# Buffers that wait by tile, combinations in other places and sooner, and a plain block first, in a two-layer decoder kernel

## The chip, the core and the metric

The kernel runs on one core of one Trainium2 chip. The core has a matrix engine (TensorE, in the profile PE, with its weight loads apart as PEld), VectorE (DVE), ScalarE (ACT), GpSimd (POOL) and SyncE (SP), which issues DMAs. DMAs are issued on SP's, ACT's and POOL's queues. The metric is the device time of one execution in microseconds (us), the median of the runs.

## The reference

Two decoder layers on 256 tokens of width 2048, in float32. Layer 0 mixes tokens with gated linear attention (GLA), layer 1 with sliding-window attention over a shared K and V. Each is followed by an MLP with a squared ReLU. Cut to what matters here:

```python
def sqrelu_mlp(h, w1, w2):          # w1: 2048 x 8192, w2: 8192 x 2048
    u = jax.nn.relu(h @ w1)
    return (u * u) @ w2
...
for layer in range(2):
    u = rmsnorm(h, norm_mix[layer])
    h = h + (gla_mixer(u, ...) if layer == 0 else swa_sink_mixer(u, ...))   # both end with  o @ w_o
    h = h + sqrelu_mlp(rmsnorm(h, norm_mlp[layer]), mlp_w1[layer], mlp_w2[layer])
```

## The kernel before

**Products in halves.** Every matrix product is made with both operands split in two: a rounded half (`wh`, `ah`) and the remainder (`wl`, `al`). Three matmuls, `ah*wh`, `ah*wl` and `al*wh`, make up one. A weight block is 512 x 512 (1 MB). It is loaded into a `ws`, `wx` or `wy` buffer; `halve` (L106) casts it on ACT to `wh` (L115) and subtracts on DVE for `wl` (L116), two instructions of each per block. `wp` holds three `ws`, four `wh` and three `wl`. A *plain* block (`Seven.plain`, L238) serves two token tiles with 24 matmuls; a *product* (`Seven.product`, L227) has 12.

**Seven products for eight.** A 2 x 2 arrangement of blocks is multiplied with seven products instead of eight (class `Seven`, L187). For that, sums of activations are formed (`combinations`, L685: four operands, each with its two halves) and sums of weight blocks. The weight sums are made in part by DMA: `load_x` (L211) loads a block in two halves into `wx`, and later adds another onto it with an accumulating DMA on POOL's queue (L216); the first load goes to SP's queue (L218). The order of the products and plain blocks is a string: a single digit is a product, two digits `ij` are a plain block of row `i` and column `j`, `e` and `a` take results out, `x` adds a sum on DVE. Product 1 needs `wx` and the activation's column block 0; plain block 31 needs column block 3.

**The order of the work.** The kernel is written for a tool that places each instruction by its priority in the order of the text, and draws every wait on buffers itself. Loads, casts and remainders of weights are moved up by `high_priority(offset=WPRI)`. Other steps are put off by hand: `later(n, fn)` (L73) runs `fn` at the n-th next `tick()`; a product has one tick, a plain block two.

**From mixer to MLP.** `residual` (L847) multiplies the mixer's output by `w_o`, column blocks 0 and 1 plain and 2 and 3 by seven products in the order `1 21 31 3 7 e 5 20 30 6 2 4`. Its operands are made by `combine_act` (L892) at ticks `COMB`. As a column block is complete, `add_to` (L823) adds it to the residual stream `xs` (L826), and `operands` (L814) turns it with PE transposes (`back`, L810) and scales it into the MLP's activation `act` (ACT L322, DVE L323). Column block 3 is complete after product 6, column block 2 after product 4, the last. `keep_act` (L906) forms the combinations that the MLP needs for every quarter, in two halves `b`, at ticks `KEEP` after the plain columns: sums `xu` (L903), differences `xe` (L688), rounded `xo` (ACT L694) and their remainders (DVE L688). It writes them to DRAM (`kept`, L912, on POOL's queue).

**The MLP.** `mlp` (L932) goes through the hidden width in four quarters `g`. In each, `fetch_sums` (L943) fetches `kept` into `cmb` on POOL's queue, two calls of `two_columns` (L949) make four column blocks of the hidden layer, and `seven` (L1052) multiplies them by `w2`. `two_columns` takes a `wx` from the pool `mp` (two buffers); `wy` is in `mp` too.

**Pools.** Buffers live in pools: `gp` and `g2` in layer 0's mixer, `sp` and `s2` in layer 1's, `mp` in the MLP. A pool opened after another is closed lies on its bytes. In the tool's default (`reuse_waits="pool"`), all tiles of the new pool wait for every user of the pools whose bytes it lands on. A `tag` is a group of buffers of one size within a pool. For a partition, in bytes: in layer 0, `mlev` 189728 to 197920 (two buffers), `z` and two `og` to 202016, four `v` to 210208, four `g` to 218400, two `oh` (with `xu`) to 222496, two `ol` (with `xe`) to 226592; `wx0`, `wgh` and `AT` below. In layer 1, `kh` and `kl` 174208 to 182400, two `qhl` 190720 to 198912, two `qTt` 198976 to 207168, two `sc` to 215360, two `po` (with `xu`) 215616 to 219712. In the MLP, two `wx` 195840 to 212224 and `wy` to 220416.

Of the kernel before, what the change touches and what calls it, by code (L numbers as in the profile page):

```python
# [8 lines left out]
F32 = mybir.dt.float32  # L9
F32R = mybir.dt.float32r  # L10
# [6 lines left out]
P = 128  # L17
# [4 lines left out]
C = 512  # L22
# [18 lines left out]
MX = 2  # L41
COMB = (1, 3)
ORDERS = "1 21 3 7 31 e 5 20 30 6 2 4", "21 1 31 3 7 e 5 20 30 6 2 4"
KEEP = 7, 10
OPS = 7, 9
SQ = (3, 2)
ATT = (5, 3), (9, 6), (10, 8), (11, 10)
# [3 lines left out]
def yoco_kernel(ctx: ExitStack, tc: tile.TileContext, x, norms, mlp_w1, mlp_w2, a_w_in, w_glr, w_gate, a_g_o, a_w_o,  # L51
                kv_w_k, kv_w_v, kv_g_k, b_w_q, b_g_q, b_sinks, b_w_o, out):
    nc = tc.nc
# [19 lines left out]
    def later(n, fn):  # L73
        due.setdefault(now[0] + n, []).append(fn)
# [112 lines left out]
    class Seven:  # L187

        def __init__(self, block, act, es, wx, wy=None):
            self.at, self.act, self.wx, self.banks = block, act, wx, {}
            self.es, self.wy = es, wy

        def block(self, i, j):
            return self.at(i, j).rearrange("(k p) n -> p k n", p=P)
# [14 lines left out]
        def load_x(self, i, j, more=True):  # L211
            with tc.high_priority(offset=WPRI):
                for n in range(2):
                    o, a = self.wx[n], self.block(i, j)[:, 2 * n:2 * n + 2]
                    if more:
                        nc.gpsimd.dma_start(out=o, in_=a, accum_op=ALU.add)  # L216
                    else:
                        nc.sync.dma_start(out=o, in_=a.bitcast(F32))  # L218

        def op(self, i):  # L220

# [195 lines left out]
    wx0 = gp.tile([P, 2, C], F32, name="wx0")  # L417
# [35 lines left out]
    g2 = ga.enter_context(tc.tile_pool(name="g2", bufs=2))  # L453
# [66 lines left out]
    AT = gp.tile([P, 3, H, P], F32, name="AT")  # L520
# [164 lines left out]
    def combinations(os, bs, us, es, sf):  # L685

        ua, ub = us
        sub = lambda o, i, j: nc.vector.tensor_sub(out=o, in0=i, in1=j)  # L688
        sub(es[:, 0], ua[:, :, P:], ub[:, :, P:])
        sub(es[:, 1], ua[:, :, :P], es[:, 0])  # L690
        sub(sf[:, 0], ub[:, :, :P], es[:, 1])
        sub(sf[:, 1], ua[:, :, :P], ua[:, :, P:])
        for o, e in zip(os, (es[:, 0], es[:, 1], sf[:, 0], sf[:, 1])):
            nc.scalar.copy(out=o[:, 0, bs], in_=e)  # L694
            sub(o[:, 1, bs], e, o.bitcast(F32)[:, 0, bs])
# [151 lines left out]
    def residual(w, act, gains, first, room, kept):  # L847
# [20 lines left out]
        for b in range(2):  # L868
            later(KEEP[b], lambda b=b: keep_act(acts[0], b, room, kept))
        v, wx = room["v"](), room["wx"]()  # L870
# [29 lines left out]
    def sums(act, bs, room):  # L900
        us = [room["u"]() for _ in range(2)]
        for c, u in enumerate(us):
            nc.vector.tensor_add(out=u, in0=act[c][0].bitcast(F32)[:, bs], in1=act[c][1].bitcast(F32)[:, bs])  # L903
        return us

    def keep_act(act, b, room, kept):  # L906

        bs = slice(2 * b, 2 * b + 2)
        os = room["o"](b)
        combinations(os, slice(0, 2), sums(act, bs, room), *(room["e"]() for _ in range(2)))  # L910
        for i, o in enumerate(os):
            nc.gpsimd.dma_start(out=kept[i // 2][:, i % 2, :, bs], in_=o.bitcast(F32))  # L912
# [3 lines left out]
    def new_kept(n):  # L916
        return [dp.tile([P, 2, 2, 4, P], F32, name=f"kept{n}{i}") for i in range(2)]

    kept = new_kept(0)

    (actm,), rm = residual(a_w_o[0], acto, (G_MLP0,), True, {
        "v": lambda: g2.tile([P, C], F32, name="vp", tag="vp", bufs=1),
        "wx": lambda: [wx0, g2.tile([P, 2, C], F32, name="wx1", tag="mlev")],
        "es": lambda: [g2.tile([P, 2, 4, P], F32R, name="cmb1", tag="mlev"),
                       wgh.rearrange("p (a k n) -> p a k n", a=2, k=4)],
        "u": lambda: g2.tile([P, 2, T], F32, name="xu", tag="oh"),
        "e": lambda: g2.tile([P, 2, 2, P], F32, name="xe", tag="ol"),
        "o": lambda b: [g2.tile([P, 2, 2, P], F32R, name="xo", tag="vg"[b], bufs=4) for _ in range(4)]}, kept)
    ga.close()


    def mlp(w1, w2, act, r, gains, kept):  # L932
        mx = ExitStack()
        mp = mx.enter_context(tc.tile_pool(name="mp", bufs=2))
        sq, nr = new_norm() if gains else (None, None)
        acts = [{} for _ in gains]
        vs = [mp.tile([P, C], F32, name=f"v{n}", bufs=1) for n in range(2)]
# [8 lines left out]
                with tc.high_priority(offset=WPRI):  # L946
                    nc.gpsimd.dma_start(out=a.bitcast(F32), in_=o)

        def two_columns(col, es, hs, put, order):  # L949


            x = mp.tile([P, 4, C], F32, name="wx", tag="wx")
            add = lambda o, i, j: nc.vector.tensor_add(out=o, in0=i, in1=j)
            sub = lambda o, i, j: nc.vector.tensor_sub(out=o, in0=i, in1=j)
            h, ef = {}, []

            def relu(o, i, t):
                nc.scalar.activation(out=o, in_=i, func=AF.Relu, scale=r[:, t:t + 1])

            def turn(j, t, h):  # L960
                tp = bank([P, 4, P], "tp")
                for k in range(4):
                    nc.tensor.transpose(out=tp[:, k, :], in_=h[:, k * P:(k + 1) * P], identity=ident)  # L963
                put(j, slice(t * P, (t + 1) * P), tp)

            def p1(p):
                h["v"] = hs("v")
                nc.scalar.mul(out=h["v"], in_=p, mul=-1.0)

            def p7(p):  # L970
                h["22"] = hs("22")
                nc.scalar.copy(out=h["22"], in_=p)

            def p5(p):
                h["21"] = hs("p5")
                nc.scalar.copy(out=h["21"], in_=p)

            def p56(p):
                x12, x21 = hs("12"), hs("21")
                v, x22, x5, h["21"] = h["v"], h["22"], h["21"], x21  # L980
                add(v, p, v)
                add(x12, ef[0], v)
                relu(x12, x12, 0)
                later(3, lambda: turn(1, 0, x12))
                sub(x22, v, x22)
                add(x22, ef[1], x22)
                relu(x22, x22, 1)
                later(3, lambda: turn(1, 1, x22))
                sub(x21, x5, v)

            def p2(p):
                relu(h["v"], p, 0)
                later(1, lambda: turn(0, 0, h["v"]))

            def p4(p):
                add(h["21"], p, h["21"])
                relu(h["21"], h["21"], 1)
                later(1, lambda: turn(0, 1, h["21"]))

            z = Seven(lambda i, j: w1[i * C:(i + 1) * C, col[j]:col[j] + C], act, es,  # L1000
                      [x[:, 2 * i:2 * i + 2] for i in range(2)],
                      lambda: mp.tile([P, 4, C], F32, name="wy", tag="wy", bufs=1))
            z.run({"p1": p1, "p7": p7, "ef": lambda e, f: ef.extend((e, f)), "p5": p5, "p56": p56, "a": p2, "c": p4},
                  order)

# [188 lines left out]
        for g in range(4):  # L1194
            w = w2[g * D:(g + 1) * D]
            us, uf = {}, {}
            if g:
                op = new_ops()
            sums, es = new_sums()
            fetch_sums(sums)  # L1200
            if g == 0:
                op = new_ops()
            for c in range(2):
                uf[c] = mp.tile([P, 4, T], F32, name="u", tag="u")

            def put_uf(c, tt, tp, uf=uf):
                nc.scalar.activation(out=uf[c][:, :, tt], in_=tp, func=AF.Square)

            two_columns([g * D + c * C for c in range(2)], es, h_ops(), put_uf,
                        "1 21 3 7 5 31 x 20 e 6 2 30 a 4" if g else "1 31 21 3 7 5 x 20 e 6 2 30 a 4")  # L1210
            for odd in range(2):
                later(OPS[odd], lambda odd=odd, op=op, uf=uf: combine(op, odd, uf))

            def put_us(j, tt, tp, us=us):
                c = 3 - j
                if c not in us:
                    us[c] = new_act()
                ah, al, _ = us[c]
                nc.scalar.activation(out=ah[:, :, tt], in_=tp, func=AF.Square)
                nc.scalar.activation(out=tp, in_=tp, func=AF.Square)  # L1220
                nc.vector.tensor_sub(out=al[:, :, tt], in0=tp, in1=ah.bitcast(F32)[:, :, tt])

            two_columns([g * D + c * C for c in (3, 2)], es, h_rest(), put_us, "1 21 3 7 5 31 x 20 e 6 2 30 a 4")
            for n in range(2):
                seven(w, n, op, us, g, acts, gains, sq, nr)
# [4 lines left out]


    sa = ExitStack()
    sp = sa.enter_context(tc.tile_pool(name="sp", bufs=1))
    s2 = sa.enter_context(tc.tile_pool(name="s2", bufs=2))

    own = sp.tile([P, P], F32, name="own")
    nc.gpsimd.memset(own, 1.0)
# [26 lines left out]
    kh = sp.tile([P, 4, NT, P], F32R, name="kh")  # L1264
    kl = sp.tile([P, 4, NT, P], F32R, name="kl")
# [146 lines left out]
    for g in range(4):  # L1412
# [3 lines left out]
    kept = new_kept(1)  # L1416
# [3 lines left out]
        "es": lambda: [s2.tile([P, 2, 4, P], F32R, name="cmb1", tag="qTt") for _ in range(2)],  # L1420
        "u": lambda: s2.tile([P, 2, T], F32, name="xu", tag="po"),
        "e": lambda: s2.tile([P, 2, 2, P], F32, name="xe", tag="pv"),
        "o": lambda b: [a[:, i] for a in [s2.tile([P, 2, 2, 2, P], F32R, name="xo", tag="qhl") for _ in range(2)]
                        for i in range(2)]}, kept)
    sa.close()
    mlp(mlp_w1[1], mlp_w2[1], actm, rm, (), kept)


# [41 lines left out]
```

## Time and profile before

| what | value |
|---|---|
| time, median of 3 runs | 2047.86 us (2046.93 to 2048.99) |
| the profiled execution | 2049.62 us |
| its span, first to last instruction | 2047.9 us |
| mean granted PE clock | 0.993 |
| busy: PE, DVE, ACT, POOL | 2007.1, 1774.1, 1320.7, 203.6 us |
| moved by DMA | 444.02 MB, mean 217 GB/s |

A row of the order in time has the start in us from the span's start, the time taken, engine, line, operation, written tile `<-` read tile, and shape; `x2` counts merged instructions; the bracket is the engine's idle time before it and what ended that. `SPq` is the queue on which SyncE issues DMAs. In a list of waits the columns are: us in total, number, longest. In a table of stretches each engine has busy us and a count, followed by the granted PE clock, the busy share of the DMA engines and GB/s. Matmul ends are modelled, and a wait for several things is put down to the one that came last.

### The profile page before, as it was taken

The page shows a single profiled execution, that of the slowest core. Times are in us where ns is not written, and L with a number is a line of the kernel's source. Part 1 is how long each engine was busy: PE and PEld are TensorE (multiplying, and loading weights), DVE is VectorE, ACT ScalarE, POOL GpSimd, SP SyncE. Part 2 cuts the span into 40 slices and gives each one's busy share as a digit, 9 for nine tenths or more (in the row PEclk, how much of TensorE's full clock was granted, in tenths as well). Part 3 has the DMA queues.
Part 4 walks back from the last instruction along what each step waited for, and adds up shares of the span by engine and source line. Part 5 has one row for each costly group of instructions (what it writes and reads, how often), then busy time and mean ns, then how long its engine had stood idle before and what let it go on. Part 6 is the DMA issues. An engine that isn't in the chain of part 4 may idle for free.

```text
span 2047.9 us, 25613 instructions
## 1 busy us (share of the span) xinstructions
PE 2007.1 (98%) x9578; PEld 1656.0 (81%) x9578; DVE 1774.1 (87%) x1928; ACT 1320.7 (64%) x1732; POOL 203.6 (10%) x223
## 2 busy tenths in 40 slices
PE   9999999989999999999999999979999999999999
PEld 9988888768878888888887878758888888888887
DVE  6688787879889998989999677979898988998998
ACT  6746666557656657656766677647666656755765
POOL 1251110100000000000001121110000000000000
PEclk9999999989999999999999999989999999999999
DMA  8445776787787687778765543787678678778764
GB/s 284 144 155 179 222 206 206 212 268 218 227 248 244 207 270 226 231 254 253 205 206 166 165 144 125 198 273 225 227 250 241 207 255 255 212 227 256 233 220 129
DMA packets 223372, 444.02 MB, mean 217 GB/s; under 512 B 8352, under 2 KB 18864, under 8 KB 221200
## 3 DMA queue, kind: packets, MB, share of 16 engines
q1 hardware_dynamic: 194752, 376.73, 53.9%
q0 software_dynamic: 25408, 63.79, 15.4%
q10 hardware_dynamic: 3088, 1.88, 0.3%
q8 instruction: 75, 1.23, 0.2%
q14 instruction: 49, 0.40, 0.1%
HBM read 436.07 MB, written 6.29 MB: 216 GB/s over the span
## 4 chain that ended last, share of the span: by engine, by line
PE 66%; issue 16%; DVE 8%; DMA 7%; ACT 3%; POOL 1%; ACTq 0%; SPq 0%; POOLq 0%; DVEq 0%
PE acc L82 49%; PE ms L82 11%; DMA wx<-in_mlp_w_dram 4%; PE tp L82 4%; DVE wl L116 3%; DMA wx<-in_b_w_o_dram 1%; PE tp L963 1%; ACT wh L115 1%; ACT sc L1350 1%; DMA wx<-in_a_w_o_dram 1%; POOL wx L216 0%; DMA ws<-in_a_w_in_dram 0%; PE tp L1282 0%; DVE xs L1107 0%; DVE st L1344 0%
## 5 line engine op out<-in xcount | busy, mean ns | idle before, releaser
L82 PE MATMUL acc<-wh,act 128*128 128x512 f32 x3104 | 1000.3, 395 | 13.1 <-ACT wh L115 12.5
L115 ACT CAST wh<-ws 128x1024 fp32r<-128x1024 f32 x568 | 594.3, 1052 | 335.3 <-PE acc L82 213.7
L116 DVE TENSOR_TENSOR wl<-ws,wh 128x1024 fp32r<-128x1024 f32 x568 | 697.0, 1240 | 91.5 <-ACT wh L115 87.6
L82 PEld LDWEIGHTS acc<-wh,act 128*128 128x128 f32 x3104 | 583.7, 189 | 138.7 <-ACT wh L115 13.6
L82 PE MATMUL acc<-wl,act 128*128 128x512 f32 x1552 | 607.9, 392 | 8.0 <-DVE wl L116 8.0
L115 ACT CAST wh<-wx 128x1024 fp32r<-128x1024 f32 x288 | 302.6, 1052 | 214.8 <-PE acc L82 139.6
L116 DVE TENSOR_TENSOR wl<-wx,wh 128x1024 fp32r<-128x1024 f32 x288 | 347.0, 1220 | 87.5 <-ACT wh L115 84.1
L82 PEld LDWEIGHTS acc<-wl,act 128*128 128x128 f32 x1552 | 292.8, 189 | 70.7 <-DVE wl L116 11.8
L82 PE MATMUL ms<-wh,act 128*128 128x512 f32 x512 | 166.4, 393 | 0.0
L82 PE MATMUL acc<-wh,ops 128*128 128x512 f32 (+1 forms) x392 | 123.3, 386 | 0.1
L82 PE MATMUL acc<-wh,op 128*128 128x512 f32 x384 | 123.4, 389 | 0.0
L82 PEld LDWEIGHTS ms<-wh,act 128*128 128x128 f32 x512 | 96.2, 188 | 19.5
L82 PE MATMUL tp<-wh,cmb 128*128 128x512 f32 x320 | 105.1, 389 | 0.0
L82 PE MATMUL ms<-wl,act 128*128 128x512 f32 x256 | 99.7, 389 | 0.0
L82 PE MATMUL acc<-wh,cmb 128*128 128x512 f32 x296 | 96.1, 391 | 0.0
L82 PE MATMUL acc<-act,wh 128*128 128x256 f32 x512 | 95.5, 285 | 0.5 <-ACT wh L380 0.5
L1070 POOL DMA_DIRECT2D wx<-in_mlp_w_dram x16 | 20.6, 1290 | 652.9 <-DVE wl L116 652.9
L82 PEld LDWEIGHTS acc<-wh,ops 128*128 128x128 f32 x392 | 73.2, 188 | 15.0 <-ACT wh L115 0.6
L82 PEld LDWEIGHTS acc<-wh,op 128*128 128x128 f32 x384 | 72.1, 188 | 14.9
L82 PEld LDWEIGHTS acc<-act,wh 128*128 128x128 f32 x512 | 80.6, 191 | 1.0 <-ACT wh L380 0.8
L82 PE MATMUL acc<-wl,ops 128*128 128x512 f32 (+1 forms) x196 | 76.3, 389 | 3.1 <-DVE wl L116 3.1
L116 DVE TENSOR_TENSOR wl<-wy,wh 128x1024 fp32r<-128x1024 f32 x64 | 76.0, 1219 | 1.3 <-ACT wh L115 1.3
(284 smaller groups left out, 2494.0 us busy)
## 6 DMA issues: line engine op xcount, KB each, us to landing
ws<-in_mlp_w_dram SPq DMA_DIRECT2D x192, 1024.0 KB, 5.6
ws<-in_a_w_in_dram SPq DMA_DIRECT2D x42, 1024.0 KB, 5.1
wy<-in_mlp_w_dram SPq DMA_DIRECT2D x32, 1024.0 KB, 6.2
cmb<-kept POOLq DMA_DIRECT2D x16, 1024.0 KB, 5.4
wx<-in_mlp_w_dram SPq DMA_DIRECT2D x32, 512.0 KB, 6.0
wx<-in_mlp_w_dram POOLq DMA_DIRECT2D x32, 512.0 KB, 6.8
wx<-in_mlp_w_dram SPq DMA_DIRECT2D x16, 1024.0 KB, 5.3
wx<-in_mlp_w_dram POOLq DMA_DIRECT2D x16, 1024.0 KB, 9.5
```

The lines of the kernel that those rows point to most:

```text
L82: nc.tensor.matmul(o, lhsT=l, rhs=r, start=start, stop=stop, **kw)
L115: nc.scalar.copy(out=wh[:, js, :o], in_=w)
L116: nc.vector.tensor_sub(out=wl[:, ks, :o], in0=w, in1=wh.bitcast(F32)[:, js, :o])
L963: nc.tensor.transpose(out=tp[:, k, :], in_=h[:, k * P:(k + 1) * P], identity=ident)
L1070: nc.gpsimd.dma_start(out=ws, in_=block(i, j).rearrange("(k p) n -> p k n", p=P), accum_op=ALU.add)
L1350: nc.scalar.activation(out=sc[:, h], in_=sc[:, h], func=AF.Exp, bias=nmx[:, h:h + 1], scale=f[:, h:h + 1], accum_out=su[:, h:h + 1])
```

## The change

- The pools `mp`, `sp` and `s2` are opened with `reuse_waits="tile"`: each of their tiles waits only for the users of earlier tiles on its own bytes.
- In layer 0, `keep_act`'s `xo` are taken from tag `g` for both halves (before: `v` for the first, `g` for the second), and the second half of residual's `wx` is a part of `AT` (before: an `mlev` buffer).
- In layer 1, `keep_act`'s `xo` are parts of `kh` and `kl` (before: `qhl` buffers).
- `keep_act` runs at ticks 5 and 8 (before: 7 and 10).
- In the first quarter of each MLP, the first `two_columns` starts with plain block 31 and then product 1 (before: product 1, then 31). There the first load of `wx` is issued on POOL's queue (before: SP's).

```diff
-KEEP = 7, 10
+KEEP = 5, 8
...
-        def __init__(self, block, act, es, wx, wy=None):
+        def __init__(self, block, act, es, wx, wy=None, queue=nc.sync):
             self.at, self.act, self.wx, self.banks = block, act, wx, {}
-            self.es, self.wy = es, wy
+            self.es, self.wy, self.queue = es, wy, queue
...
                     if more:
                         nc.gpsimd.dma_start(out=o, in_=a, accum_op=ALU.add)
                     else:
-                        nc.sync.dma_start(out=o, in_=a.bitcast(F32))
+                        self.queue.dma_start(out=o, in_=a.bitcast(F32))
...
-        os = room["o"](b)
+        os = room["o"]()
...
-        "wx": lambda: [wx0, g2.tile([P, 2, C], F32, name="wx1", tag="mlev")],
+        "wx": lambda: [wx0, AT.rearrange("p a h n -> p (a h n)")[:, :2 * C].rearrange("p (a n) -> p a n", a=2)],
...
-        "o": lambda b: [g2.tile([P, 2, 2, P], F32R, name="xo", tag="vg"[b], bufs=4) for _ in range(4)]}, kept)
+        "o": lambda: [g2.tile([P, 2, 2, P], F32R, name="xo", tag="g", bufs=4) for _ in range(4)]}, kept)
...
-        mp = mx.enter_context(tc.tile_pool(name="mp", bufs=2))
+        mp = mx.enter_context(tc.tile_pool(name="mp", bufs=2, reuse_waits="tile"))
...
-        def two_columns(col, es, hs, put, order):
+        def two_columns(col, es, hs, put, order, queue=nc.sync):
...
-                      lambda: mp.tile([P, 4, C], F32, name="wy", tag="wy", bufs=1))
+                      lambda: mp.tile([P, 4, C], F32, name="wy", tag="wy", bufs=1), queue)
...
-                        "1 21 3 7 5 31 x 20 e 6 2 30 a 4" if g else "1 31 21 3 7 5 x 20 e 6 2 30 a 4")
+                        "1 21 3 7 5 31 x 20 e 6 2 30 a 4" if g else "31 1 21 3 7 5 x 20 e 6 2 30 a 4",
+                        nc.sync if g else nc.gpsimd)
...
-    sp = sa.enter_context(tc.tile_pool(name="sp", bufs=1))
-    s2 = sa.enter_context(tc.tile_pool(name="s2", bufs=2))
+    sp = sa.enter_context(tc.tile_pool(name="sp", bufs=1, reuse_waits="tile"))
+    s2 = sa.enter_context(tc.tile_pool(name="s2", bufs=2, reuse_waits="tile"))
...
-        "o": lambda b: [a[:, i] for a in [s2.tile([P, 2, 2, 2, P], F32R, name="xo", tag="qhl") for _ in range(2)]
-                        for i in range(2)]}, kept)
+        "o": lambda: [a[:, 2 * i:2 * i + 2] for a in (kh, kl) for i in range(2)]}, kept)
```

## The prediction

> **What bounds the kernel now.** I read the page first, then what TensorE (PE) waits for, then the engines' order in time at the places where it waits.
>
> ```profile
> PE 2007.1 (98%) x9578; PEld 1656.0 (81%) x9578; DVE 1774.1 (87%) x1928; ACT 1320.7 (64%) x1732; POOL 203.6 (10%) x223
> ```
>
> PE is busy for 98% of the span, so an edit that leaves its work alone can only win what PE waits and what it loses to a lower clock. The list of PE's waits shows nearly all of it at two places of one kind: where residual() hands over to mlp(), once per layer. I call them T1 (around 410 us) and T2 (around 1352 us). Columns: us in total, times, longest. First 400 to 424, then 1340 to 1366:
>
> ```profile
> PE acc L82 <- ACT wh L115: 5.7, 1, 5.7
> PE acc L82 <- DVE wl L116: 3.4, 4, 1.6
> PE tp L810 <- DVE act L323: 2.1, 1, 2.1
> PE tp L810 <- DVE xs L826: 1.1, 1, 1.1
> ```
>
> ```profile
> PE acc L82 <- ACT wh L115: 6.8, 1, 6.8
> PE acc L82 <- DVE wl L116: 3.5, 3, 1.9
> PE tp L810 <- DVE act L323: 2.1, 1, 2.1
> ```
>
> That is 12.3 us at T1 and 12.4 us at T2, 24.7 in all. A second loss is the clock after a wait. In the table of stretches PEclk is the granted clock:
>
> ```profile
> 424.00:436.00 12.00, 12.00 (x49) 9.75 (x48) 10.61 (x10) 7.12 (x10) 3.24 (x3) 0.89 1.08 318
> 1340.00:1352.00 12.00, 8.98 (x31) 6.64 (x30) 12.00 (x20) 4.75 (x10) 2.89 (x4) 0.86 0.61 213
> ...
> 1364.00:1376.00 12.00, 11.48 (x42) 9.05 (x42) 10.40 (x11) 8.46 (x11) 3.76 (x3) 0.80 1.07 296
> ```
>
> The missing clock times 12 us gives 1.3, 1.7 and 2.4 us, 5.4 together. What can be won at most is therefore 24.7 + 5.4 = 30.1 us.
>
> The longest wait is named as ACT, but ACT waits too. PE and ACT at T1, in order of time (start, us, engine, line; in brackets the idle time before):
>
> ```profile
> 411.07 1.06 PE L810 MATMUL tp<-ident,xs 128*128 128x128 f32 x8 [1.07 <-DVE xs L826]
> 414.29 1.94 PE L810 MATMUL tp<-ident,xs 128*128 128x128 f32 x8 [2.15 <-DVE act L323]
> 421.97 0.80 PE L82 MATMUL acc<-wh,act 128*128 128x512 f32 x1 [5.74 <-ACT wh L115]
> ```
>
> ```profile
> 420.87 1.04 ACT L115 CAST wh<-wx 128x1024 fp32r<-128x1024 f32 x1 [6.28 <-DMA wx<-in_mlp_w_dram]
> 421.82 0.83 ACT L322 ACTIVATE act<-tp,gT 128x256 fp32r<-128x256 f32 x2
> ```
>
> PE has finished residual's products at about 410.0; the MLP's first product starts at 421.97, since its weight block wx has only just landed. SyncE issued that block here, at T1 and T2:
>
> ```profile
> 412.56 0.88 SPq L218 DMA_DIRECT2D wx<-in_mlp_w_dram  x2
> ```
>
> ```profile
> 1353.57 0.88 SPq L218 DMA_DIRECT2D wx<-in_mlp_w_dram  x2
> ```
>
> Both stand right behind residual's last work. The pool mp lies on the bytes of the pools closed before it, and by pool each of its tiles waits for every user of those. At T2 PE does the same:
>
> ```profile
> 1348.30 0.78 PE L82 MATMUL acc<-wl,act 128*128 128x512 f32 x1 [1.90 <-DVE wl L116]
> ...
> 1363.57 0.80 PE L82 MATMUL acc<-wh,act 128*128 128x512 f32 x1 [6.80 <-ACT wh L115]
> ```
>
> The waits for wl come from VectorE (DVE), which is full at the end of residual. DVE at T2:
>
> ```profile
> 1337.46 1.23 DVE L116 TENSOR_TENSOR wl<-wx,wh 128x1024 fp32r<-128x1024 f32 x1 [1.46 <-ACT wh L115]
> 1338.60 0.69 DVE L903 TENSOR_TENSOR xu<-act 128x512 f32<-128x512 f32 x1
> ...
> 1345.69 1.43 DVE L688 TENSOR_TENSOR xo<-xe,xo 128x256 fp32r<-128x256 f32 x4
> 1347.03 2.35 DVE L116 TENSOR_TENSOR wl<-wx,wh 128x1024 fp32r<-128x1024 f32 x2
> ...
> 1350.50 1.28 DVE L826 TENSOR_TENSOR xs<-vp,xs 128x512 f32<-128x512 f32 x2
> ```
>
> The second half of keep_act (two xu, four xe, four xo: about 2 x 0.6 + 8 x 0.34 = 3.9 us) runs just ahead of the last product's wl and of the additions that complete column block 3 (L826).
>
> **Waits by tile.** Now a tile of mp waits only for users of its own bytes. By the addresses of the kernel before (the change adds no tag and no size), mp's first wx lies on the second mlev buffer, the og buffers and one v buffer in layer 0. The change takes residual's wx1 out of mlev (to AT) and the xo of keep_act's first half out of v (to g). What is left on those bytes is the xr of turn_x, last read here:
>
> ```profile
> 359.57 0.49 PE L800 MATMUL tp<-ident,xr 128*128 128x128 f32 x3
> ```
>
> In layer 1 the first wx lies on a qhl buffer and the two qTt buffers. The xo leave qhl for kh and kl; the qTt hold operands 2 and 3 of residual's seven products, read for the last time here:
>
> ```profile
> 1325.23 0.39 PE L82 MATMUL acc<-wh,cmb 128*128 128x512 f32 x1
> ```
>
> So the first wx can be issued some 52 us earlier at T1 (412.6 - 360) and 28 us earlier at T2 (1353.6 - 1325.2). A landing takes under 10 us at both places (412.56 to 420.87), so wx is there before residual ends and the waits of 5.7 and 6.8 us for it go. The second wx and wy stay on SyncE and lie on g, oh and sc, po buffers that residual uses to its end; SyncE has by then issued the three ws blocks that fit, so nothing useful stands behind them. For sp and s2 I take zero: what they set free is POOL's masks and constants, which no engine waits for at that place.
>
> **The queue.** The first wx moves from SyncE to POOL, past residual's accumulating loads, the writes of keep_act and the fetch of cmb. At T1 it stands alone, 20 us ahead of the next accumulating loads. At T2 it comes just behind them:
>
> ```profile
> 1324.55 2.43 POOL L216 DMA_DIRECT2D wx<-in_b_w_o_dram  x2 [20.58 <-DVE wl L116]
> ```
>
> They feed the cast ahead of 1337.46, which is on the path. If 1 MB more shares the DMA engines at the 318 GB/s of 424 to 436, they land up to 1.05/0.318 = 3.3 us later; if it queues behind them, 0. A gain I exclude, since nothing is taken off. I take 1 us, nearer to the second, as both stand in one queue.
>
> Does POOL as issuer cost something? Loads of 1 MB from both queues, with the median time to landing last:
>
> ```profile
> wy<-in_mlp_w_dram SPq DMA_DIRECT2D x32, 1024.0 KB, 6.2
> cmb<-kept POOLq DMA_DIRECT2D x16, 1024.0 KB, 5.4
> ```
>
> By these rows nothing. The Trainium skill, page "SBUF — State Buffer", section "SBUF: two separate sides", speaks against the move: it says that descriptors of a load issued from POOL are written through a port that VectorE can lock, so that the load stands still while VectorE works. By that rule wx would come later here, beside a DVE that is full; it is given a chance below.
>
> **Combinations sooner (KEEP 7, 10 to 5, 8).** Two ticks are one plain block or two products. No work goes away. DVE fills idle time with it that it has while it waits for casts: 1.46 us at T2 (row 1337.46), and between 385 and 400:
>
> ```profile
> DVE wl L116 <- ACT wh L115: 3.6, 2, 2.1
> ```
>
> So column block 3 is complete 1.46 us sooner at T2 and 3.6 us sooner at T1, and the last products' wl no longer stand behind xo, so that the 3.4 and 3.5 us of PE's waits for wl mostly go. In the middle of residual the earlier combinations run beside wl that are ahead of PE; wl has priority, and each combination holds DVE for 0.34 to 0.6 us, so I take nothing for it.
>
> **Plain block 31 first.** It needs no wx, only a ws block already loaded, but column block 3's operand act[3], which residual forms at its very end. So what is late next is the way from DVE's additions to act[3]. DVE at T1:
>
> ```profile
> 410.85 0.68 DVE L873 TENSOR_TENSOR xs<-xs,vp 128x512 f32<-128x512 f32 x1
> 411.63 0.69 DVE L826 TENSOR_TENSOR xs<-acc,xs 128x512 f32<-128x512 f32 x1
> 412.25 0.92 DVE L323 SCALAR_TENSOR_TENSOR act<-tp,gT,act 128x256 fp32r<-128x256 f32 x2
> ```
>
> The additions to block 3 end as L873 starts, at 410.9; the first slice of act[3] is ready at 412.25 + 0.46 = 412.7: 1.8 us for transposes, scaling and remainder. The two wl of block 31 (2.35 us, the price of row 1347.03) may stand ahead of the additions or behind them.
>
> **The sum.**
> - T1: 410.9 - 3.6 + (0 to 2.35) + 1.8 = 409.1 to 411.5 for the MLP's first matmul, instead of 421.97: 10.5 to 12.9, middle 11.7.
> - T2: 1350.50 + 1.28 = 1351.8; 1351.8 - 1.46 + (0 to 2.35) + 1.8 = 1352.1 to 1354.5, instead of 1363.57: 9.1 to 11.5, middle 10.3.
> - Clock: a wait of some 3 to 4 us stays at each place, and with it the slow start of the MLP (1.3 and 2.4 us); the 1.7 us before 1352 go with the wait at 1348.30.
> - The accumulating loads at T2: -1.
>
> 11.7 + 10.3 + 1.7 - 1 = 22.7 us. The profiled execution took 2049.62 us with a span of 2047.9; 2049.62 - 22.7 = 2026.9. The median of the runs lies 1.76 below that execution (2047.86), which gives 2025. Nothing should be given back later: the MLP's loads, which now crowd the DMA engines (share 1.08 and 1.07 in the rows above), are spread over a longer time, and DVE, busy for 87% of the span, has room to catch up 2 us.
>
> **Rivals.**
> - *wx is late all the same*, because POOL's queue puts it behind the writes of keep_act, or its bytes hold another late user. Then block 31 alone fills the wait. Twelve matmuls take 2.72 us:
>
> ```profile
> 1385.85 2.72 PE tp L82 x12
> ```
>
>   so its 24 take 5.4, and both places together win 10.9: 2049.62 - 10.9 - 1.76 = 2037. For it: POOL works in order, and keep_act's writes wait for DVE. Against it: the bytes are free so early that the load should be ahead of them. Chance 0.10, and 0.03 more for the page's rule, by which the load would be starved with the same result; the rows of wy and cmb speak against that.
> - *Nothing changes*: the allocator moves other tiles onto those bytes, or waits by tile are not applied, and PE runs the product first as before. Then only the earlier combinations count, 0 to 4 us: about 2046. Chance 0.08.
> - *Slower*: ACT works in order, and at 421.82 the row above shows scaling for act standing behind a cast that waits for wx. If the same happens to act[3], block 31 cannot start before wx either. With wx issued on POOL behind keep_act's writes and the fetch, later than 412.56 and 1353.57 (that is the point from which it decides) by some 2 us, and the scaling and remainder (0.83 + 0.46) behind it, each place loses 3 to 4 us: about 2049.62 + 7 - 1.76 = 2055. Chance 0.07.
> - *All of it goes*, the waits and the slow clock: 2049.62 - 30.1 - 1.76 = 2018. This is the lower end of the forecast's own range.
>
> **How the numbers follow.** The forecast, 2018 to 2033, has a chance of 0.68; wx late 0.13; a smaller gain in between for other reasons 0.04. The range of 2018 to 2038 holds these; above it lie no change and slower with 0.15. About 0.2%, or 4.1 us, is what a measurement of this kernel can tell from no change. Faster by more: 0.85; same: 0.08; slower: 0.07.
>
> **What would show it.** Right: the first wx is issued on POOL's queue near 360 and 1326; the cast of wx no longer waits for a DMA; PE's waits between the last product of residual and the MLP's first matmul shrink to 3 to 4 us at each place, named DVE act or xs; no xo stands ahead of the last wl. Wrong, in the step of the loads: a wait for wx of several us after block 31. Wrong, in the combinations: new waits for wl between 365 and 395 or 1305 and 1340. Wrong as a whole: the MLP's first matmul of layer 0 later than 416 after as much work as before, or the rest of the span longer by what the two places win.

## The result, and the profile after

| | before | after |
|---|---|---|
| median of 20 runs each, same chip | 2047.9 us (2044.42 to 2050.26) | 2043.31 us (2040.71 to 2047.47) |
| the profiled execution | 2049.62 us | 2041.34 us |
| its span | 2047.9 us | 2039.6 us |

The ratio is 0.9979, with an interval of 0.9973 to 0.9986: the change saves 0.14 to 0.27%, about 4.6 us, and not 22.7. The profiled execution of before lies 1.7 us above its median and that of after 2.0 below, so the two traces differ by 8.3 us, more than the medians do.

PE's line on the page of after, and its waits from 400 to 440 and from 1330 to 1380 (us in total, times, longest):

```profile
PE 2007.4 (98%) x9578; PEld 1656.9 (81%) x9578; DVE 1774.5 (87%) x1928; ACT 1321.1 (65%) x1732; POOL 203.4 (10%) x227
```

```profile
PE acc L82 <- ACT wh L115: 3.6, 2, 3.4
PE tp L810 <- DVE xs L826: 2.4, 1, 2.4
PE tp L82 <- DVE xs L872: 1.8, 1, 1.8
...
PE acc L82 <- ACT wh L115: 4.4, 2, 4.0
PE tp L810 <- DVE xs L826: 2.9, 1, 2.9
PE tp L82 <- DVE xs L872: 1.0, 1, 1.0
```

PE's work is the same to 0.3 us. At T1 the waits sum to 7.8 us (12.3 before), at T2 to 8.3 (12.4). The waits for wl at residual's end are gone, and a wait of a new kind has come (L872: DVE's addition that reads product 5 out of its accumulator, bank D, which product 6 needs). A wait for ACT's wh is still the longest, but it has another place. PE in order of time; first the MLP's first matmul of layer 0 and of layer 1, and behind each the place where PE stops next:

```profile
413.36 0.50 PE L82 MATMUL acc<-wh,act 128*128 128x512 f32 x1
...
424.89 0.79 PE L82 MATMUL acc<-wh,act 128*128 128x512 f32 x1 [3.43 <-ACT wh L115]
...
1348.94 0.50 PE L82 MATMUL acc<-wh,act 128*128 128x512 f32 x1
...
1362.56 0.50 PE L82 MATMUL acc<-wh,act 128*128 128x512 f32 x1 [3.97 <-ACT wh L115]
```

The MLP starts at 413.36 instead of 421.97: 8.6 us won. Then PE runs through block 31 and the first six matmuls of product 1, and stops between the halves of product 1. What is left after that is read from one and the same piece of work in both chains, layer 1's attention between T1 and T2 (start, us, what):

```profile
1267.60 8.25 PE acc L82 x36
```

```profile
1262.73 8.25 PE acc L82 x36
```

The first is before, the second after: 4.87 us remain of T1's 8.6. T2's start is 1363.57 - 1348.94 = 14.63 us earlier, of which 4.87 come from T1, so T2 wins 9.8; the two spans differ by 8.3, so 3.4 of T2's 9.8 remain at the end. In these two traces 18.4 us are won at the two starts and about 10 given back.

**What stands in front of the second half of product 1.** ACT and DVE of after at T1:

```profile
415.58 1.05 ACT L115 CAST wh<-wx 128x1024 fp32r<-128x1024 f32 x1
...
423.43 0.47 ACT L322 ACTIVATE act<-tp,gT 128x256 fp32r<-128x256 f32 x1 [2.85 <-DVE act L323]
423.80 1.03 ACT L115 CAST wh<-wx 128x1024 fp32r<-128x1024 f32 x1
```

```profile
417.80 0.48 DVE L323 SCALAR_TENSOR_TENSOR act<-tp,gT,act 128x256 fp32r<-128x256 f32 x1
420.31 2.29 DVE L277 TENSOR_TENSOR ws<-ws,wy 128x2048 f32<-128x2048 f32 x1 [2.03 <-DMA wy<-in_mlp_w_dram]
422.52 0.87 DVE L323 SCALAR_TENSOR_TENSOR act<-tp,gT,act 128x256 fp32r<-128x256 f32 x2
```

Read it backwards. PE waits for the second cast of wx (423.80). That cast does not wait for its load; it stands on ACT behind the four scalings of act[2] (L322), which product 1 does not need. The last scaling waits for a remainder on DVE that reads the same bank (L323), and those remainders stand on DVE behind the sum for product 7 (L277), which waits 2.03 us for wy. So a load that product 7 needs holds product 1, through two engines that work in order. The Trainium skill, page "TensorE: Matmul & The Clock Gate", states in its table of specs that the queues of ScalarE and VectorE are strictly first in, first out; these rows agree, with ACT idle for 2.85 us although a cast of loaded data is next.

**The loads.** POOL's queue of after at T1:

```profile
397.10 1.45 POOL L912 DMA_DIRECT2D kept<-xo  x2 [9.43 <-DVE xo L688]
399.24 1.45 POOL L912 DMA_DIRECT2D kept<-xo  x2 [0.70 <-DVE xo L688]
400.69 0.73 POOL L218 DMA_DIRECT2D wx<-in_mlp_w_dram  x1
402.19 0.57 POOL L947 DMA_DIRECT2D cmb<-kept  x1 [0.77 <-DMA kept<-xo]
403.40 0.54 POOL L947 DMA_DIRECT2D cmb<-kept  x1 [0.64 <-DMA kept<-xo]
403.93 0.72 POOL L218 DMA_DIRECT2D wx<-in_mlp_w_dram  x1
...
1337.71 0.73 POOL L218 DMA_DIRECT2D wx<-in_mlp_w_dram  x1
```

The first wx goes out at 400.69 and not near 360, at T2 at 1337.71 and not near 1326: it stands behind the last writes of `keep_act`, in an order that is fixed when the program is made. Even so the first cast (415.58) waits for no DMA. Whether wx, had it gone out near 360, would have let wy land earlier was not tried.

**The clock**, in stretches of 12 us (PEclk is the column behind POOL's); the first row is before, the others are after:

```profile
420.00:432.00 12.00, 9.57 (x32) 7.42 (x33) 8.66 (x10) 9.09 (x12) 3.76 (x3) 0.72 1.07 319
...
396.00:408.00 12.00, 10.23 (x38) 7.95 (x37) 11.33 (x14) 7.01 (x11) 5.44 (x8) 0.86 0.96 352
420.00:432.00 12.00, 8.42 (x24) 6.08 (x23) 9.42 (x9) 6.27 (x8) 1.39 (x2) 0.72 0.71 154
...
1335.00:1347.00 12.00, 8.84 (x36) 6.41 (x35) 12.00 (x15) 5.26 (x5) 5.27 (x8) 1.00 0.91 304
1347.00:1359.00 12.00, 10.71 (x46) 8.33 (x46) 6.67 (x13) 6.57 (x16) 1.98 (x2) 0.86 1.04 393
1359.00:1371.00 12.00, 7.99 (x28) 6.35 (x29) 9.20 (x10) 6.86 (x8) 1.23 (x1) 0.86 0.73 164
```

Missing clock times 12 gives, for after, 1.7, 3.4, 0, 1.7 and 1.7, 8.5 us in all (a part of it lies in waits, where it costs nothing). The 3.4 us at T1's stop are not new: before has the same 0.72 in the same stretch.

### The profile page after: what moved, and what is told of

Read it like the earlier page. It is cut to its first block, busy times and chain, and to the rows that moved or that the text cites. A ratio compares the mean times of both kernels' runs of the same rounds, so it can differ in the third digit from the quotient of the medians.

```text
span 2039.6 us, 25579 instructions
## 1 busy us (share of the span) xinstructions
PE 2007.4 (98%) x9578; PEld 1656.9 (81%) x9578; DVE 1774.5 (87%) x1928; ACT 1321.1 (65%) x1732; POOL 203.4 (10%) x227
## 4 chain that ended last, share of the span: by engine, by line
PE 78%; issue 7%; DVE 7%; DMA 5%; ACT 3%; POOL 1%; ACTq 0%; SPq 0%; POOLq 0%; DVEq 0%
PE acc L82 59%; PE ms L82 12%; PE tp L82 5%; DVE wl L116 3%; DMA wx<-in_mlp_w_dram 2%; PE tp L963 1%; DMA wy<-in_mlp_w_dram 1%; ACT sc L1351 1%; ACT wh L115 1%; DMA kept<-xo 1%; DVE ws L277 1%; DVE sc L1361 0%; PE tp L1283 0%; DVE st L1345 0%; DMA cmb<-kept 0%
## 5 line engine op out<-in xcount | busy, mean ns | idle before, releaser
L115 ACT CAST wh<-wx 128x1024 fp32r<-128x1024 f32 x284 | 298.5, 1053 | 196.1 <-PE acc L82 145.8
L116 DVE TENSOR_TENSOR wl<-wx,wh 128x1024 fp32r<-128x1024 f32 x284 | 342.1, 1219 | 67.6 <-ACT wh L115 63.8
L1070 POOL DMA_DIRECT2D wx<-in_mlp_w_dram x16 | 20.6, 1290 | 653.1 <-DVE wl L116 653.1
L216 POOL DMA_DIRECT2D wx<-in_mlp_w_dram x32 | 38.9, 1230 | 390.0 <-DVE wl L116 390.0
```

What stands on the lines that cost most here:

```text
L115: nc.scalar.copy(out=wh[:, js, :o], in_=w)
L116: nc.vector.tensor_sub(out=wl[:, ks, :o], in0=w, in1=wh.bitcast(F32)[:, js, :o])
L1070: nc.gpsimd.dma_start(out=ws, in_=block(i, j).rearrange("(k p) n -> p k n", p=P), accum_op=ALU.add)
```

## The experiments

Line numbers of experiments run up to 17 higher, since lines are added. Each was timed beside the kernel before on its chip; the last columns are PE's longest wait inside or just ahead of product 1, at T1 and T2 ("none": no wait of 0.5 us or more there).

| run | what differs from the changed kernel | median us | ratio to before, interval | T1 | T2 |
|---|---|---|---|---|---|
| a_again | nothing | 2043.52 | 0.9985 [0.9976, 0.9994] | 2.9 | 5.4 |
| d1 | waits by pool again | 2048.51 | 1.0007 [0.9998, 1.0015] | 5.4 | 5.5 |
| d2 | combinations at 7, 10 again | 2059.52 | 1.0064 [1.0051, 1.0077] | 10.7 | 12.7 |
| o1 | old places | 2047.12 | 0.9996 [0.9987, 1.0005] | 10.2 | 4.7 |
| d3 | product 1 first, wx on SP | 2038.39 | 0.9955 [0.9941, 0.9969] | 2.7 | 3.6 |
| q1 | block 31 first, wx on SP | 2040.61 | 0.9973 [0.9963, 0.9984] | none | 0.8 |
| q2 | product 1 first, wx on POOL | 2049.17 | 1.0003 [0.9994, 1.0012] | 4.9 | 6.1 |
| l1 | second pair's wx later on SP | 2043.75 | 0.9977 [0.9968, 0.9987] | 3.6 | 4.1 |
| e1 | sum for product 7 behind act[2] | 2041.1 | 0.9968 [0.9955, 0.998] | 1.5 | 2.6 |
| c1 | product 1's second cast ahead as well | 2032.48 | 0.993 [0.9917, 0.9942] | none | none |
| p1 | c1, and product 5's addition ahead | 2031.68 | 0.9918 [0.9905, 0.9932] | none | none |
| p2 | p1, and block 31's remainders late | 2028.6 | 0.9902 [0.9889, 0.9916] | none | none |

The theory after the reading above was A: the order on ACT and DVE makes the stop. The rivals: the loads come too late or in one burst (L), or one of the other parts costs what the rest wins.

**The sum for product 7 behind act[2] (e1).** `formed` holds the last scaling and remainder that were written, those of act[2].

```diff
-            with tc.high_priority(offset=WPRI):
+            with ExitStack() as order:
+                order.enter_context(tc.high_priority(offset=WPRI))
+                if self.queue is nc.gpsimd:
+                    order.enter_context(tc.issue_after(formed[1].ins))
                 nc.vector.tensor_add(out=b12, in0=b12, in1=self.y)
```

> The changed kernel, with one edit: in the first pair of columns of each MLP the weight sum of product 7 (DVE, ws += wy) is ordered behind the remainders of act[2], on DVE's queue alone; no other engine's order differs. Theory A (the new wait is one of order: the sum waits for wy at the head of DVE's queue, three remainders of act[2] stand behind it, ACT waits for them and holds back the second cast of product 1): PE's waits of 3.4 and 4.0 us in the middle of product 1 go, and with them some of the slow clock behind them, 8 to 11 us faster than the changed kernel, some 2034 beside 2048 for the kernel before. Rival Q (the loads are too many, PE waits for wy one step later, at product 3 or 7): at most 2 us faster than the changed kernel, and a wait of PE of 3 us or more after product 1 stays.

Measured: 2041.1 us, where theory A gave 2034. By the ratios it is some 2 to 3 us better than the changed kernel, but the intervals overlap, so a gain is not shown. ACT and DVE show what else stood in the way:

```profile
421.69 0.47 ACT L325 ACTIVATE act<-tp,gT 128x256 fp32r<-128x256 f32 x1 [0.55 <-DVE act L326]
422.07 1.03 ACT L115 CAST wh<-wx 128x1024 fp32r<-128x1024 f32 x1
```

```profile
422.60 2.28 DVE L280 TENSOR_TENSOR ws<-ws,wy 128x2048 f32<-128x2048 f32 x1
424.80 1.22 DVE L116 TENSOR_TENSOR wl<-wx,wh 128x1024 fp32r<-128x1024 f32 x1
```

At T1 nobody waits for wy any more (at T2 the sum still does, for 1.00 us). But the cast still stands behind all scalings of act[2], which go at the pace of PE's transposes, and now the sum stands ahead of product 1's second remainder. PE stops for 1.16, 0.45 and 1.47 us at T1, 3.1 in all where the changed kernel had 3.6. As it stood, the theory named only a part of the cause.

**One part of the change undone at a time (d1, d2, d3, o1).** Waits by pool again in `mp`, `sp` and `s2` (every engine's order stays the same):

> The changed kernel with waits by pool again in all three pools. Every engine's order is that of the changed kernel, only waits differ. If waits by tile are what was won (the step of the prediction): the first wx and wy are issued only when residual has ended, near 412 and 1350, and the time is 5 to 10 us above the changed kernel, at or above that of the kernel before. Rival (block 31 covers the landing of wx, and wy lands late either way): within 2 us of the changed kernel.

Measured: 2048.51. Without waits by tile the rest of the change is worth nothing, so within this set they carry about 5 us. POOL and ACT:

```profile
413.38 0.73 POOL L218 DMA_DIRECT2D wx<-in_mlp_w_dram  x1 [11.83 <-ACT junk L830]
```

```profile
420.58 1.05 ACT L115 CAST wh<-wx 128x1024 fp32r<-128x1024 f32 x1 [4.61 <-DMA wx<-in_mlp_w_dram]
```

The combinations late again:

```diff
-KEEP = 5, 8
+KEEP = 7, 10
```

> The changed kernel with KEEP = 7, 10 again. By the prediction the earlier combinations were worth the 6.9 us of waits for wl: 5 to 7 us above the changed kernel. Rival (the earlier combinations only moved the wait: the copy of product 5 out of its bank now stands behind them on DVE, PE waits 1.8 and 1.0 us for the bank, and a slow clock follows): within 2 us of the changed kernel, with the waits for wl back and those for L872 gone.

Measured: 2059.52, 16 us worse than the changed kernel and slower than before, which neither theory had. POOL's load of wx now goes out at 408.94, behind later writes, wy at 412.22 comes together with the other loads, and the sum for product 7 waits for wy and holds the same chain for far longer (the row below). That the crowding makes wy late is read from these times and was not tried apart.

```profile
429.71 2.29 DVE L277 TENSOR_TENSOR ws<-ws,wy 128x2048 f32<-128x2048 f32 x1 [10.51 <-DMA wy<-in_mlp_w_dram]
```

Block order and queue undone:

```diff
-                        "1 21 3 7 5 31 x 20 e 6 2 30 a 4" if g else "31 1 21 3 7 5 x 20 e 6 2 30 a 4",
-                        nc.sync if g else nc.gpsimd)
+                        "1 21 3 7 5 31 x 20 e 6 2 30 a 4" if g else "1 31 21 3 7 5 x 20 e 6 2 30 a 4",
+                        nc.sync)
```

> The changed kernel with the order 1 31 and SyncE's queue for the first wx again; waits by tile, other places and KEEP = 5, 8 stay. By the prediction block 31 first is worth little where wx is early: within 3 us of the changed kernel, with product 1 filling the wait for act[3]. Rival (wx is late on SyncE's queue, behind the weight blocks): 4 to 8 us above the changed kernel, with PE waiting for the cast of wx.

Measured: 2038.39. Its ratio, 0.9941 to 0.9969, lies below both of the changed kernel's. The two edits together cost some 5 us, though each was to help. There is no stop of 0.5 us or more inside product 1 here. PE waits 2.7 and 3.6 us ahead of it, and here it is the load: SP issued wx at 405.20, and ACT's first cast waits 3.21 us for it, until 416.31.

The places of before (`xo` in `v`, `g` and `qhl`, residual's `wx1` in `mlev`), all else as changed:

> The changed kernel with the combinations' tiles and the sum buffer of layer 0 and 1 at their old places; waits by tile, sooner combinations, block order and POOL's load stay. Theory P (the places are free room for the sooner combinations, and the old ones make them wait for v and g of the attention): a wait on VectorE or ScalarE at the combinations and 2044 to 2050. Rival (the old places are free as early): 2040 to 2043, as the changed kernel.

Measured: 2047.12, so the places are worth some 3 us by the ratios (its interval overlaps with that of a_again, not with the first one of the changed kernel), but not as either theory had it: the combinations wait for nothing new (DVE's one wait for xo is 1.9 us in both). It is the MLP's wx that lies on residual's `wx1` again, and goes out only after that one's last remainder; wy then takes until 427.63:

```profile
406.64 0.73 POOL L218 DMA_DIRECT2D wx<-in_mlp_w_dram  x1 [6.29 <-DVE wl L116]
```

```profile
427.63 2.29 DVE L277 TENSOR_TENSOR ws<-ws,wy 128x2048 f32<-128x2048 f32 x1 [9.21 <-DMA wy<-in_mlp_w_dram]
```

**Block order and queue apart (q1, q2), beside the changed kernel (a_again) and the cast ahead (c1).**

> The changed kernel itself, as the base for the three runs beside it. All theories: 2041 to 2044, 4 to 6 us under the kernel before.

> The changed kernel with the first product's load of w back on SP, block 31 still first. Theory Q (POOL's fixed order, the kept writes and the fetches around the two halves of the load, is what costs): about 2038.5, as with block order and queue both undone (2038.4), and the casts of product 1 stand earlier on ScalarE. Theory O (block 31 in front puts act[2]'s scalings and its casts ahead of product 1's second cast, on whatever queue the load is): 2041 to 2044 and a stop of 3 to 4 us inside product 1 again.

> The changed kernel with product 1 in front of block 31 again, the load of w still issued by POOL (near 401 and 404 us in layer 0). Theory Q: 2041 to 2044, since the load is as late as in the changed kernel. Theory O: about 2038.5, with no stop inside product 1; MLP's first matmul then comes about 4 us later than in the changed kernel.

Measured: q1 2040.61, q2 2049.17, a_again 2043.52. Both theories fall in part. With POOL as issuer there is a stop whichever block is first, and with product 1 first it is the longer one (4.9 and 6.1 us). With SP there is none over 0.8 us inside product 1. But the load is not what PE waits for in q2: the sum for product 7 stands ahead of act[2]'s remainders again.

```profile
419.06 2.29 DVE L277 TENSOR_TENSOR ws<-ws,wy 128x2048 f32<-128x2048 f32 x1 [2.52 <-DMA wy<-in_mlp_w_dram]
```

```profile
427.30 2.28 DVE L277 TENSOR_TENSOR ws<-ws,wy 128x2048 f32<-128x2048 f32 x1
429.50 0.47 DVE L323 SCALAR_TENSOR_TENSOR act<-tp,gT,act 128x256 fp32r<-128x256 f32 x1
```

The first is q2, the second q1. There the sum comes behind product 1's remainders and waits for nothing, but it still stands ahead of one remainder of act[2], for which PE waits 2.46 us in block 21. The tool places the same instructions otherwise when wx is issued by another engine; why it does was not tried. Whether q1 is better than the changed kernel is not settled by its time, since the intervals overlap.

Product 1's second cast ahead of act[2]'s second half, and the sum for product 7 behind product 1's second remainder (c1). `made` holds the last cast and remainder of a weight block, and act[2]'s second half is scaled a tick after its transposes:

```diff
+        if wait:
+            later(1, lambda: scale(acts, gains, c, b, tp, made[0]))
...
+                    if cast is not None:
+                        order.enter_context(tc.high_priority(offset=WPRI))
+                        order.enter_context(tc.issue_after(cast.ins))
                     scaled(a[c], kt, tp[:, j], g[:, c * 4 + kt:c * 4 + kt + 1])
...
+                if self.queue is nc.gpsimd:
+                    order.enter_context(tc.issue_after(self.made[1].ins))
                 nc.vector.tensor_add(out=b12, in0=b12, in1=self.y)
```

> The changed kernel in which the second half of act[2] is scaled only behind product 1's second cast, and p7's sum stands on VectorE behind product 1's second remainder (a few other instructions of that pair change places with it). Theory O: the stop of 3.4 and 4.0 us inside product 1 goes with the slow clock behind it, 2035 to 2037. Rival (the load's second half lands only then): the cast waits for its DMA instead, 2040 to 2043.

Measured: 2032.48, 11.0 us better than a_again on the same chip (some 8 to 14 by the ratios) and better than the theory asked. PE's waits from 400 to 440 and from 1330 to 1380:

```profile
PE tp L816 <- DVE xs L842: 2.9, 1, 2.9
PE tp L82 <- DVE xs L888: 1.8, 1, 1.8
...
PE tp L816 <- DVE xs L842: 2.8, 1, 2.8
PE tp L82 <- DVE xs L888: 1.0, 1, 1.0
```

The wait for ACT is gone at both places, and no load ahead of it was moved. ACT now has:

```profile
418.62 1.04 ACT L117 CAST wh<-wx 128x1024 fp32r<-128x1024 f32 x1
```

The cast runs at 418.62, 5.2 us earlier, without a wait for a DMA: the data was there before the changed kernel used it. Compared with the trace of a_again, matmul by matmul, c1 wins 5.6 us at T1 and 6.6 at T2, the slow clock behind the stops included; it was 1.3 ahead before T1, and loses some 4.5 again in the rest of the two MLPs, where the tool placed other instructions otherwise too. So the order at the two places is worth at least the 10 us that the result's reading found given back; that the medians differ by nearly the same is in part chance.

**The burst of loads (l1).** The second pair's 1 MB of wx on SP goes behind the first pair's last block; no other engine's order differs.

```diff
+                if (i, j) == (3, 0):
+                    self.mark[:] = [d]
...
+                if not more and self.after:
+                    order.enter_context(tc.issue_after(self.after[0].ins))
```

> The changed kernel with the second pair's load of w (1 MB on SP at 410.7 and 1346.2 us) behind the first pair's last block in SP's queue; no other engine's order differs. Theory L (the burst of loads near 405 to 420 us makes wy land late, and the sum for product 7 wait 2.0 and 3.0 us for it): that wait goes and 2037 to 2039. Theory O (the order on ScalarE and VectorE holds product 1's second cast): 2040 to 2043, since act[2]'s scalings still stand ahead of it.

Measured: 2043.75, no change. The sum still waits 2.61 us for wy, which was issued at 409.73:

```profile
421.12 2.29 DVE L283 TENSOR_TENSOR ws<-ws,wy 128x2048 f32<-128x2048 f32 x1 [2.61 <-DMA wy<-in_mlp_w_dram]
```

That one load is not what makes wy late, or not enough to matter. Fetching less of `cmb` then was not tried.

**What the other steps missed (p1, p2).** Product 5's addition ahead of the combinations, on top of c1:

```diff
+        def soon(p):
+            with tc.high_priority(offset=WPRI):
+                add(x21, p)
...
-... "p5": lambda p: add(x21, p), "p56": p56,
+... "p5": soon, "p56": p56,
```

> The run with product 1's second cast ahead, and in the residuals the addition of product 5 out of bank D put ahead of the combinations too (a few remainders and one sum near it change places). Theory D (the sooner combinations keep that addition, so bank D, 1.8 and 1.0 us in front of product 6, and about 2 us of half pace behind it): 2028 to 2030. Rival (VectorE is full until the residual's end, and the time is only moved to the wait for the additions ahead of act[2]'s transposes): 2031 to 2034.

Measured: 2031.68, where the rival was to be. The waits for bank D are gone, but PE waits 0.6 and 1.5 us for wl in their place and 3.1 and 2.9 us for the additions. Against c1 the intervals overlap.

Block 31's two remainders behind the additions, on top of that (`after` is the last addition that product 6 feeds):

```diff
-                made[:] = h, nc.vector.tensor_sub(...)
+                with tc.issue_after(after.ins) if after else ExitStack():
+                    made[:] = h, nc.vector.tensor_sub(...)
```

> The same, with block 31's two remainders behind the four additions after product 6 on VectorE as well. Theory W (the two remainders, 2.3 us, in front of the additions make the waits of 2.9 us for act[2]'s transposes): those waits fall below 1 us and the time by 3 to 5 us more. Rival (31's first products then wait for the remainders or for act[2]'s instead, VectorE having no gap there): within 1.5 us of the run beside it.

Measured: 2028.6, 3.1 us better than p1 on the same chip (four executions of each, and the intervals of the ratios overlap). PE's waits from 400 to 440 and from 1330 to 1380, and the clock at both places:

```profile
PE acc L82 <- DVE wl L119: 1.6, 3, 1.0
PE tp L817 <- DVE xs L843: 0.8, 1, 0.8
PE acc L82 <- DVE act L330: 0.8, 1, 0.8
...
PE acc L82 <- DVE wl L119: 0.8, 2, 0.6
PE acc L82 <- DVE act L330: 0.8, 1, 0.8
PE tp L817 <- DVE xs L843: 0.6, 1, 0.6
```

```profile
408.00:420.00 12.00, 10.29 (x51) 7.97 (x52) 10.59 (x18) 9.39 (x19) 2.94 (x3) 1.00 1.03 404
1335.00:1347.00 12.00, 10.52 (x50) 7.83 (x49) 11.30 (x18) 8.26 (x18) 2.37 (x4) 1.00 0.98 378
```

No wait is over 1 us, and the clock is full at both places. The MLP starts at:

```profile
409.99 0.73 PE L82 MATMUL acc<-wh,act 128*128 128x512 f32 x2
```

This version beats both kernels: 19.7 us below before on its chip, with the change's own parts in it and three edits of order. That this is near the 22.7 of the forecast does not bear the forecast out, since it needed these edits.

## Why the prediction was wrong, point by point

- **Where the time is lost** (two places, 24.7 us of waits and 5.4 of clock): right, and nearly all that was won or given back lies there. The clock's part was read too low: its 1.3 us at T1 come from a stretch that starts at 424, while the clock was 0.72 from 420 to 432 and the MLP began at 421.97.
- **The step that failed is "Nothing should be given back later".** The start of the MLP moved by 18.4 us where 22.0 were forecast; some 10 of these, in the two traces, were lost within the next 20 us. The working looked at whether wx is there, and for block 31 at the way to act[3]. It didn't ask what stands between the two casts of product 1 on ACT, and between the scalings' remainders on DVE. c1 shows that this order, with the slow clock behind it, costs some 11 us.
- **wx "can be issued some 52 us earlier".** Wrong: the bytes were free, but the load stands behind the last writes of `keep_act` on POOL, 400.69 at T1 and 1337.71 at T2 (11.9 us earlier than before at T1, and 11.0 at T2 with T1's 4.87 taken off). The prediction had the reason in hand, in its rival of a late wx: POOL works in order, and `keep_act`'s writes wait for DVE. Against it stood only that the bytes are free early, which does not move a load past the writes. For wx itself this cost nothing, since the casts wait for no load. The 1 us taken off for the accumulating loads at T2 did not arise either: wx went out 18 us behind them.
- **POOL as issuer, by the rows nothing.** Right for the transfer. The Trainium skill, page "SBUF — State Buffer", section "SBUF: two separate sides", states its rule for VectorE operations that run in a mode with two ports, a condition that the prediction left out. The trace shows no such stall here: DVE was busy for 11.33 of the 12 us from 396, with TENSOR_TENSOR rows alone, and wx, issued at 400.69 and 403.93, landed 4.7 and 9.9 us later, before its casts ran. Whether other operations would stall it no run here shows. But moving the load changed the order of other engines (q2 against d3: by the ratios some 10 us), a cost that was not in the working.
- **Combinations sooner.** Right that the waits for wl of 3.4 and 3.5 us go. "I take nothing" for the middle of residual was 1.8 and 1.0 us: the addition of product 5 now stands behind combinations on DVE, and product 6 waits for its bank. Why sooner combinations are needed at all was missed: with the load on POOL they set when it can go (d2, 16 us).
- **The MLP's first matmul.** T1: forecast 409.1 to 411.5, measured 413.36. Block 31's two remainders stand ahead of the additions, the upper end of the 0 to 2.35 us, and the term of 3.6 us was too large: of the idle time that DVE was to fill, 1.86 us stayed, about what the start came later than 411.5 (the row below, DVE of after). T2: 1348.94, with T1's 4.87 us added 1353.8, within 1352.1 to 1354.5. With p2's order the matmul comes at 409.99 at T1.

```profile
396.37 0.42 DVE L688 TENSOR_TENSOR xo<-xe,xo 128x256 fp32r<-128x256 f32 x1 [1.86 <-ACT xo L694]
```

- **The clock.** The 1.7 us before 1352 went, but 1.7 (bank D) and 1.7 (1347 to 1359) came. At T1's stop the clock is what it was before (0.72 from 420 to 432).
- **The rivals.** Later loads of wx: the load was late, but its cast did not wait for it. "Slower" had the right kind of mechanism, a head of ACT's queue that holds the rest, but the wrong pair: not scalings behind a cast that waits for wx, but a cast behind scalings that wait, through DVE, for wy. It was also held to be possible only if wx were late.
- **All parts as a set.** Taking back waits by tile, places or sooner combinations costs 3 to 16 us each; taking back block order and queue together wins some 5. Without waits by tile (d1) or the places (o1) the rest is no better than before. None of the parts was tried alone.

## What to carry to other kernels

When an edit lets work start sooner, follow the in-order engines past the first instruction that starts sooner, to the second and third that the same product needs, and list what stands ahead of each and what that waits for. An engine that is idle with loaded data next in its queue is the sign to look for: there an edit of the order can win time without any earlier load. And look at the order again after moving a DMA to another engine's queue, since the tool that places instructions may place others differently.

## What was not expected of the hardware

- The clock after a wait does not go by the wait's length alone. In after, PE waited 1.77 us for bank D and ran at half pace from 400.50 to about 404 (0.43 us from one matmul to the next, otherwise 0.23); in c1 the same wait of 1.77 us, at the same place, was followed by full pace, and so was one of 1.76 us in a_again, the same kernel as after. The granted clock from 396 to 408 was 0.86 in after and 1.00 in the other two.
- The DMA engines moved 393 GB/s (after, from 1347) and 404 (p2, from 408) for 12 us, with SP and POOL both issuing. The 1 MB of wy that after issued at 410.32 and 1345.70 took 10 to 12 us to land, against a median of 6.3 over the kernel; at T1 it took 17.4 in d2 and 18.3 in o1.
